# Down projection of 40 of 44 ffn tiles by one level of Strassen's algorithm, its products placed between units of gate and up

## The chip, the cores and the metric

The kernel runs on one core of a Trainium2 chip. The metric is the device time of one execution in microseconds; for the kernel before it is the median of three runs. A profile of one execution stands beside it. The engines are TensorE (PE, with its weight loads as PEld), VectorE (DVE), ScalarE (ACT), GpSimd (POOL) and SyncE (SP), which here only issues loads and stores.

## The reference

The kernel computes one encoder block on 512 tokens of width 2048 in float32: a norm, an input projection, two kinds of token mixing (Fourier and gated), an output projection, a second norm, a SwiGLU ffn of width 5632 and a last norm.

```python
h = rmsnorm(x, norm_mix); z = h @ w_in
y_f = fourier_mixer(z[..., :1024], w_fourier)
u, v = split(gelu(z[..., 1024:]))
y_g = spatial_gating_mixer(u, v, g_sgu, w_spatial, b_spatial)
x = x + concatenate([y_f, y_g], -1) @ w_out
h2 = rmsnorm(x, norm_ffn)
x = x + (silu(h2 @ w_gate) * (h2 @ w_up)) @ w_down
return rmsnorm(x, norm_final)
```

The change touches the last projection, `@ w_down`, and the order of the work around it.

## The kernel before

**Precision.** Every float32 product is carried by three passes of a shorter format. An operand is split into hi, a cast on ScalarE, and lo, the rest, a subtraction on VectorE (`split`, L169 to L171, and `weights`, L66 to L78). `mm3` (L80 to L84) issues hi times hi, one hi times lo, and lo times hi into the same bank; so its three lines carry nearly all matmuls in the profile.

**Weights.** All large weights come in units of 128x1024 (512 KB). `weights` loads a unit into a tile called raw, and splits it into hi and lo. Each of the three has three buffers, which all units share in turn.

**Stages ahead of the ffn.** The input projection (stages a, v and u), the mixing, and the output projection (stage o) run ahead of it. The residual x lies in eight slots of the pool `spool`, 24 slots of 4 KB a partition; `x2c(m, n)` is its block of token tile m (128 tokens, four of them) and column block n (512 columns, four of them). The normalized input of the ffn, transposed, is kept as 16 pairs h2hi and h2lo.

**The ffn.** Its width is 44 tiles of 128. `gate_up(f)` (L486) makes one tile of the activation, transposed: gate is 16 k tiles of 3 matmuls into one bank, two units of weights; then up in the same way. VectorE scales gate by `rg`, the reciprocal norm of each token, ScalarE takes the tanh, VectorE forms the product with it; up is scaled by `ru`, half of rg, and GpSimd multiplies both (L493 to L498). The tile is split into hi and lo (L500).

**Down.** Tiles are taken in groups of four (`GROUPS`, L35): for each of four column blocks two units of w_down are loaded, and for each of four token tiles `down` (L505) accumulates four tiles in one bank, 12 matmuls, which VectorE adds to x at L511. The groups are ten of four tiles and two of two. `gate_up` runs one tile ahead of the group's down. The last group's weights are split into slots of their own; its sixteen blocks are followed by the squares on ScalarE, the product with norm_final on GpSimd, the last norm and the stores (L536 to L554).

**What sets the order.** SP's queue is kept as the code writes it. On the other engines a planner puts the instructions in an order of its own, which keeps the dependencies; each engine then executes its queue in that order. A tile waits until a buffer of its pool is free. The banks of the accumulator are eight, all from one pool.

Of the kernel before, what the change touches and what calls it, by code (L numbers as in the profile page):

```python
# [16 lines left out]
P = 128  # L17
D = 2048  # model width
S = 512  # tokens
KT = D // P  # k tiles of the model width  # L20
NT = S // P  # token tiles
HEADS = 8  # fourier heads, and gmlp heads
GW = HEADS * P  # width of a head group
DFF = 5632
FT = DFF // P  # tiles of the ffn width
EPS = 1e-6
U = 1024  # columns of a unit of weights

# the tile of u behind which v is ready for the gate
# [3 lines left out]
# ffn tiles per accumulation of the down projection; the last group is small, so that  # L33
# little is left to do behind the last matmul
GROUPS = [4] * 10 + [2, 2]  # L35
# [3 lines left out]
def encoder_block(ctx, tc, a, out):  # L39
    """The block on one core.  # L40

    A float32 product is carried by float32r passes: an operand is hi + lo exactly, hi its
    leading 12 bits and lo the other 12, and hi*hi + hi*lo + lo*hi is accumulated in float32.
    """
# [3 lines left out]
    # loads and stores in the order written here  # L48
# [4 lines left out]
    spool = ctx.enter_context(tc.tile_pool(name="s", bufs=24))  # L53
# [12 lines left out]
    def weights(src, name, pieces=1):  # L66
        """A unit of weights, as hi and lo."""
# [12 lines left out]
    def mm3(ps, lhs, rhs, first, last):  # L80
        """ps += lhs.T @ rhs, both as (hi, lo)."""
        mm(ps, lhs[0], rhs[0], start=first, stop=False)  # L82
        mm(ps, lhs[0], rhs[1], start=False, stop=False)  # L83
        mm(ps, lhs[1], rhs[0], start=False, stop=last)  # L84

# [4 lines left out]
    # the tensor engine's clock rises with its use: keep it at work until the first operands are there  # L90
# [9 lines left out]
    def rsqrt(dst, ssq, scale, shape, name):  # L100
        """dst = 1 / sqrt(ssq * scale + eps), with a Newton step."""
# [39 lines left out]
    def by_token(pss, units, nk, lhs, name, per_k=None, then=()):  # L141
        """Four banks, one for each token tile: sum over k of lhs(k).T @ the unit's columns.
        then[kk] is other work, to be issued behind unit kk."""
# [15 lines left out]
    def by_feature(ps, units, nk, rhs, name):  # L159
        """One bank: the transpose of rhs times 128 columns of weights."""  # L160
# [12 lines left out]
    def pair(name, width=U):  # L173
        """hi and lo of `width` columns."""
        if width == U:
            return slot(name + "_hi", F32R), slot(name + "_lo", F32R)
        t = slot(name, F32R, (P, 2, S))
        return t[:, 0, :], t[:, 1, :]

# [4 lines left out]
    yf = []  # mixed features, transposed, as (hi, lo)  # L184
# [15 lines left out]
    def fourier_classes(av, n, scaled):  # L200
        """The sums over the four token tiles that a DFT of 512 as 4 x 128 needs."""
# [25 lines left out]
    def fourier_tokens(h):  # L227
        u, v, y0, y2 = (both(x, head_columns(h)) for x in cls[h // 4])
        # real and imaginary parts of the DFT over the tokens, [feature, frequency]:
        # re of 4m+1, re of 4m+2, re of 4m | im of 4m, im of 4m+2, im of 4m+1  # L230
# [10 lines left out]
    def fourier_features(h):  # L241
        # over the head's features, and its weights
# [7 lines left out]
        for sign, op in ((1, ALU.add), (-1, ALU.subtract)):  # L250
            # frequencies 4m+1 and their negatives
# [23 lines left out]
    def fourier_weights(n):  # L275
        """cos and sin of the head features' DFT, times the heads' weights."""
# [9 lines left out]
    def token_squares():  # L286
        """1 / rms by token, on the token's partition."""
# [5 lines left out]
    def token_squares_everywhere():  # L293
        """1 / rms by token, on every partition."""
# [18 lines left out]
    # hT is made as it is needed  # L313
# [21 lines left out]
    def gelu2(z, s, dst):  # L335
        """dst = 2 gelu(z), by tanh; s holds z squared."""
# [32 lines left out]
    # of v, where v2 = 2 v  # L369
# [10 lines left out]
    # v's place, once vn is there  # L380
# [85 lines left out]
    rg = const.tile([P, S], F32, name="rg")  # L466
    ru = const.tile([P, S], F32, name="ru")

    def ffn_scales():
        """1 / rms by token, on every partition."""  # L470
# [6 lines left out]
        nc.vector.tensor_scalar_mul(ru, rg, 0.5)  # L477

# [4 lines left out]
    fss = const.tile([P, NT, 4], F32, name="fss")  # L483
    act = [None] * FT

    def gate_up(f):  # L486
        pg, pu = bank(f"g{f}"), bank(f"up{f}")
        by_feature(pg, a["w_gate"][f], KT, lambda k: h2[k], f"g{f}")
        if f == 0:
            ffn_scales()  # L490
        t = slot(f"ft{f}", F32, (P, 2, S))
        z, s = t[:, 0, :], t[:, 1, :]
        nc.vector.tensor_mul(z, pg, rg)  # L493
        nc.scalar.activation(s, z, AF.Tanh, scale=0.5)
        nc.vector.scalar_tensor_tensor(z, s, 1.0, z, op0=ALU.add, op1=ALU.mult)
        by_feature(pu, a["w_up"][f], KT, lambda k: h2[k], f"up{f}")
        nc.vector.tensor_mul(s, pu, ru)
        nc.gpsimd.tensor_tensor(out=z, in0=z, in1=s, op=ALU.mult)  # L498
        act[f] = pair(f"act{f}", S)
        split(z, act[f])  # L500

    def down_units(f0, size, n):
        return [weights(a["w_down"][(f0 + 2 * j) // 2][n], f"d{f0}_{n}_{j}") for j in range(size // 2)]

# [124 lines left out]
```

## Time and profile before

| what | value |
| --- | --- |
| median of 3 runs | 1940.79 us (1940.61 to 1940.95) |
| span of the profiled execution, first to last instruction | 1938.5 us |
| mean granted TensorE clock | 0.997 |
| read from HBM, written | 191.98 MB, 4.19 MB |
| DMA, share of 16 engines | 30% |
| loads of w_down | 84 + 4 of 512 KB |

The device time of the profiled execution itself is not recorded, only its span; the median of the runs is 2.3 us above it. In the profile's groups each row has a line, an engine, an operation, its tiles, a shape and a count; then the busy time in us, the mean of one in ns, and how long the engine sat idle just ahead of them and what ended that. TensorE overlaps its matmuls: a single one is shown with 389 ns, while they start about every 0.227 us, so times on TensorE are taken from the starts. Tiles whose names differ only in a number are one row: d is down, g gate, up up, act the split activation.

### The profile page before, as it was taken

How to read it: one execution, taken by the hardware profiler on the slowest of the kernel's cores; microseconds unless marked ns; L12 is line 12 of the kernel's file. 1: busy time of each engine (PE TensorE's matmuls, PEld its weight loads, DVE VectorE, ACT ScalarE, POOL GpSimd, SP SyncE). 2: the span in 40 equal slices, each digit the busy share in tenths (PEclk: the TensorE clock that was granted, in tenths of full speed). 3: DMA queues.
4: the chain of work that ended last, by engine and by line, in shares of the span. 5: the costliest groups of instructions: out<-in, count | busy, mean ns of one | idle time of the engine just before them, and what ended most of it. 6: DMA issues, size and time to landing. Idle time of an engine off the chain costs nothing.

```text
span 1938.5 us, 20697 instructions
## 1 busy us (share of the span) xinstructions
PE 1919.9 (99%) x8610; PEld 1593.7 (82%) x8610; DVE 866.2 (45%) x1006; ACT 544.1 (28%) x684; POOL 124.2 (6%) x96
## 2 busy tenths in 40 slices
PE   9999999999999999999999999999999999999996
PEld 8888888888888888888888888888888888888885
DVE  7555663333434334343444343443433433434447
ACT  6345532223322221222212222222222122222224
POOL 5001110000000000000000000000000000000003
PEclk9999999999999999999999999999999999999998
DMA  6223224423222323323233223232232232332332
GB/s 240 95 70 108 90 74 141 142 87 119 88 98 87 109 98 98 98 91 104 89 98 98 98 87 109 87 109 98 92 100 95 94 98 98 98 98 87 106 104 94
DMA packets 55965, 197.51 MB, mean 102 GB/s; under 512 B 6592, under 2 KB 6720, under 8 KB 55872
## 3 DMA queue, kind: packets, MB, share of 16 engines
q1 hardware_dynamic: 55584, 195.15, 30.2%
q8 instruction: 67, 1.10, 0.2%
q0 software_dynamic: 288, 1.05, 0.2%
q14 instruction: 26, 0.21, 0.0%
HBM read 191.98 MB, written 4.19 MB: 101 GB/s over the span
## 4 chain that ended last, share of the span: by engine, by line
PE 97%; DVE 1%; ACT 1%; DMA 0%; issue 0%; POOL 0%; SPq 0%; ACTq 0%; DVEq 0%
PE up L83 8%; PE g L82 8%; PE g L83 8%; PE up L82 8%; PE g L84 8%; PE up L84 8%; PE d L84 8%; PE d L83 8%; PE d L82 8%; PE o L84 3%; PE o L83 3%; PE o L82 3%; PE a L82 2%; PE a L83 2%; PE a L84 2%; PE v L82 1%
## 5 line engine op out<-in xcount | busy, mean ns | idle before, releaser
L82 PE MATMUL up<-h2hi,hi_up 128*128 128x512 f32 x704 | 274.0, 389 | 0.0
L83 PE MATMUL up<-h2lo,hi_up 128*128 128x512 f32 x704 | 273.9, 389 | 0.0
L82 PE MATMUL g<-h2hi,hi_g 128*128 128x512 f32 x704 | 273.9, 389 | 0.0
L84 PE MATMUL g<-h2hi,lo_g 128*128 128x512 f32 x704 | 273.9, 389 | 0.0
L83 PE MATMUL g<-h2lo,hi_g 128*128 128x512 f32 x704 | 273.9, 389 | 0.0
L84 PE MATMUL up<-h2hi,lo_up 128*128 128x512 f32 x704 | 273.9, 389 | 0.0
L82 PE MATMUL d<-hi_d,act 128*128 128x512 f32 x672 | 261.4, 389 | 0.0
L83 PE MATMUL d<-lo_d,act 128*128 128x512 f32 x672 | 261.4, 389 | 0.0
L84 PE MATMUL d<-hi_d,act 128*128 128x512 f32 x672 | 261.4, 389 | 0.0
L511 DVE TENSOR_TENSOR x<-d,x 128x512 f32<-128x512 f32 x192 | 131.4, 687 | 160.4 <-PE d L84 159.4
L77 DVE TENSOR_TENSOR lo_up<-raw_up,hi_up 128x1024 fp32r<-128x1024 f32 x88 | 141.7, 1610 | 127.8 <-ACT hi_up L76 127.8
L76 ACT CAST hi_g<-raw_g 128x1024 fp32r<-128x1024 f32 x88 | 92.8, 1054 | 367.8 <-PE g L83 144.7
L76 ACT CAST hi_d<-raw_d 128x1024 fp32r<-128x1024 f32 x84 | 88.6, 1055 | 382.2 <-PE d L84 242.8
L77 DVE TENSOR_TENSOR lo_g<-raw_g,hi_g 128x1024 fp32r<-128x1024 f32 x88 | 107.7, 1224 | 150.7 <-ACT hi_g L76 150.6
L76 ACT CAST hi_up<-raw_up 128x1024 fp32r<-128x1024 f32 x88 | 92.8, 1054 | 272.2 <-PE up L83 140.4
L77 DVE TENSOR_TENSOR lo_d<-raw_d,hi_d 128x1024 fp32r<-128x1024 f32 x84 | 114.5, 1363 | 97.3 <-ACT hi_d L76 97.3
L84 PEld LDWEIGHTS g<-h2hi,lo_g 128*128 128x128 f32 x704 | 132.1, 188 | 27.5
L82 PEld LDWEIGHTS up<-h2hi,hi_up 128*128 128x128 f32 x704 | 132.1, 188 | 27.5
L82 PEld LDWEIGHTS g<-h2hi,hi_g 128*128 128x128 f32 x704 | 132.1, 188 | 27.4
L84 PEld LDWEIGHTS up<-h2hi,lo_up 128*128 128x128 f32 x704 | 132.1, 188 | 27.4
L83 PEld LDWEIGHTS g<-h2lo,hi_g 128*128 128x128 f32 x704 | 132.1, 188 | 27.4
L83 PEld LDWEIGHTS up<-h2lo,hi_up 128*128 128x128 f32 x704 | 132.1, 188 | 27.3
(229 smaller groups left out, 2511.6 us busy)
## 6 DMA issues: line engine op xcount, KB each, us to landing
raw_g<-in_w_gate SPq DMA_DIRECT2D x88, 512.0 KB, 3.3
raw_up<-in_w_up SPq DMA_DIRECT2D x88, 512.0 KB, 3.3
raw_d<-in_w_down SPq DMA_DIRECT2D x84, 512.0 KB, 3.3
raw_o<-in_w_out SPq DMA_DIRECT2D x32, 512.0 KB, 3.3
raw_v<-in_w_v SPq DMA_DIRECT2D x16, 512.0 KB, 3.3
raw_u<-in_w_u SPq DMA_DIRECT2D x16, 512.0 KB, 3.4
raw_a<-in_w_a SPq DMA_DIRECT2D x15, 512.0 KB, 3.5
x<-in_x SPq DMA_DIRECT2D x8, 512.0 KB, 8.0
```

Of the source, the lines that this page charges most:

```text
L76: nc.scalar.copy(hi[:, c], raw[:, c])
L77: nc.vector.tensor_sub(lo[:, c], raw[:, c], hi[:, c])
L82: mm(ps, lhs[0], rhs[0], start=first, stop=False)
L83: mm(ps, lhs[0], rhs[1], start=False, stop=False)
L84: mm(ps, lhs[1], rhs[0], start=False, stop=last)
L511: nc.vector.tensor_add(x2c(m, n), ps, x2c(m, n))
```

## The change

Of the 44 ffn tiles the first 40 are taken in ten groups of four, called quads. A quad's contribution to x is a product of a 512x512 matrix (tokens by ffn) and a 512x2048 matrix. For each half of the columns (np_, 1024 wide) both are cut into 2x2 blocks, of 256 tokens by 256 ffn and of 256 ffn by 512 columns, and the 2x2 block product is formed by seven block products in place of eight (Winograd's form of Strassen's algorithm). `quad_down` yields after each product. Ahead of it VectorE forms sums of the left blocks (tile x) and, in place, of the weight blocks (r); both operands are split into hi and lo. Product 2 accumulates into product 1's banks and product 3 into product 5's. A value of products 1 and 2 goes to one output block, of 5 to another, and so on; what several output blocks share (products 1 and 6) is summed over all quads in `usum`, and `fold` adds it to or subtracts it from three of the four output blocks once, after the last quad.

`gate_up` becomes a generator that yields after each of its four units of weights. While the units of a quad run, one product of the quad before is run after each unit but the first; so the 14 products (two halves of seven) stand between 16 units of gate and up.

The activation is no longer split by tile; it stays float32 in two slots a quad. `rg` takes the place of the earlier `rstdB`, and the factor 0.5 of `ru` goes into the instruction that reads up. w_down of a quad is loaded into slots of `spool` (`down_loads`) rather than into raw. The pool has 25 slots. norm_final is loaded after the last quad. The last four tiles keep the plain form, as two groups of two.

```diff
-GROUPS = [4] * 10 + [2, 2]
+H = S // 2
+QUADS = 10
...
-    spool = ctx.enter_context(tc.tile_pool(name="s", bufs=24))
+    spool = ctx.enter_context(tc.tile_pool(name="s", bufs=25))
...
-    rg = const.tile([P, S], F32, name="rg")
-    ru = const.tile([P, S], F32, name="ru")
+    rg = rstdB
     def ffn_scales():
...
         nc.vector.tensor_copy(rg, ps)
-        nc.vector.tensor_scalar_mul(ru, rg, 0.5)
+    fss = const.tile([P, NT, 4], F32, name="fss")
+    act = [None] * FT
+    def gate_up(f, z):
+        pg, pu = bank(f"g{f}"), bank(f"up{f}")
+        s = small.tile([P, S], F32, tag="act", bufs=1, name=f"s{f}")
+        per = U // P
+        for ps, w, name in ((pg, a["w_gate"], "g"), (pu, a["w_up"], "up")):
+            for kk in range(KT // per):
+                hi, lo = weights(w[f][kk], f"{name}{f}_{kk}")
+                for j in range(per):
+                    k = kk * per + j
+                    c = slice(j * P, (j + 1) * P)
+                    mm3(ps, (hi[:, c], lo[:, c]), h2[k], k == 0, k == KT - 1)
+                if kk == 0:
+                    yield
+            if name == "g":
+                if f == 0:
+                    ffn_scales()
+                nc.vector.tensor_mul(z, pg, rg)
+                nc.scalar.activation(s, z, AF.Tanh, scale=0.5)
+                nc.vector.scalar_tensor_tensor(z, s, 1.0, z, op0=ALU.add, op1=ALU.mult)
+            else:
+                nc.vector.scalar_tensor_tensor(s, pu, 0.5, rg, op0=ALU.mult, op1=ALU.mult)
+                nc.gpsimd.tensor_tensor(out=z, in0=z, in1=s, op=ALU.mult)
+            yield
+    ORDER = (1, 2, 5, 6, 3, 7, 4)
+    usum = [slot(f"u{np_}", F32, (P, 2, S)) for np_ in range(2)]
+    for np_ in range(2):
+        nc.gpsimd.memset(usum[np_], 0.0)
+    def out_block(k, t, np_):
+        return x2c(2 * (k // 10 - 1) + t, 2 * np_ + k % 10 - 1)
+    def down_loads(q, np_):
+        r = {}
+        for k in (11, 21, 12, 22):
+            r[k] = slot(f"w{k}_{q}_{np_}")
+            nc.sync.dma_start(r[k], a["w_down"][2 * q + k // 10 - 1][2 * np_ + k % 10 - 1])
+            yield r
+    def quad_down(q, np_, A, loads):
+        A11, A21 = A[0][:, :, :H], A[0][:, :, H:]
+        A12, A22 = A[1][:, :, :H], A[1][:, :, H:]
+        x = None
+        ps = {}
+        r = {}
+        for i in ORDER:
+            name = f"{q}_{np_}_{i}"
+            if i == 5:
+                x = slot(f"x{q}_{np_}", F32, (P, 2, H))
+                nc.vector.tensor_sub(x, A21, A22)
+            elif i == 6:
+                nc.vector.tensor_sub(x, x, A11)
+            elif i == 3:
+                nc.vector.tensor_add(x, x, A12)
+            elif i == 7:
+                nc.vector.tensor_sub(x, A11, A21)
+            X = slot(f"X{name}", F32R, (P, 2, 2, H))
+            split({1: A11, 2: A12, 4: A22}.get(i, x), (X[:, 0], X[:, 1]))
+            if i in (1, 2, 5, 6):
+                r = next(loads)
+            if i == 5:
+                nc.vector.tensor_add(r[11], r[11], r[12])
+            elif i == 6:
+                nc.vector.tensor_add(r[11], r[11], r[22])
+            elif i == 7:
+                nc.vector.tensor_add(r[12], r[12], r[22])
+            elif i == 4:
+                nc.vector.tensor_add(r[11], r[11], r[21])
+            raw = r[{1: 11, 2: 21, 5: 11, 6: 11, 3: 22, 7: 12, 4: 11}[i]]
+            hi = wpool.tile([P, U], F32R, tag="hi", name=f"hi_d{name}")
+            lo = wpool.tile([P, U], F32R, tag="lo", name=f"lo_d{name}")
+            split(raw, (hi, lo))
+            more = {2: 1, 3: 5}.get(i)
+            ps[i] = ps[more] if more else [bank(f"d{name}_{t}") for t in range(2)]
+            for j in range(2):
+                c = slice(j * S, (j + 1) * S)
+                for t in range(2):
+                    l = slice(t * P, (t + 1) * P)
+                    w = (hi[:, c], lo[:, c])
+                    p = ps[i][t]
+                    mm(p, X[:, 0, j, l], w[0], start=j == 0 and not more, stop=False, skip_group_check=True)
+                    mm(p, X[:, 0, j, l], w[1], start=False, stop=False, skip_group_check=True)
+                    mm(p, X[:, 1, j, l], w[0], start=False, stop=j == 1, skip_group_check=True)
+            for t in range(2):
+                if i in (1, 6):
+                    d = usum[np_][:, t, :]
+                else:
+                    d = out_block({2: 11, 5: 22, 3: 12, 7: 21, 4: 21}[i], t, np_)
+                nc.vector.tensor_add(d, ps[i][t], d)
+                if i == 7:
+                    d = out_block(22, t, np_)
+                    nc.vector.tensor_sub(d, d, ps[i][t])
+            yield
+    def fold():
+        for np_ in range(2):
+            for t in range(2):
+                for k in (12, 21, 22):
+                    d = out_block(k, t, np_)
+                    nc.vector.tensor_tensor(d, d, usum[np_][:, t, :], op=ALU.add if k == 21 else ALU.subtract)
+    def downs(q, A):
+        for np_ in range(2):
+            yield from quad_down(q, np_, A, down_loads(q, np_))
+    def run(work):
+        next(work, None)
+    def chain(works):
+        for w in works:
+            yield from w
+    pending = iter(())
+    for q in range(FT // 4):
+        A = [slot(f"act{q}_{i}", F32, (P, 2, S)) for i in range(2)]
+        for i, _ in enumerate(chain(gate_up(4 * q + f, A[f // 2][:, f % 2, :]) for f in range(4))):
+            if i > 0:
+                run(pending)
+        pending = downs(q, A)
+        if q == QUADS:
+            fold()
+            rest = A
     gB = [slot(f"gB{i}") for i in range(2)]
     for i in range(2):
         nc.sync.dma_start(gB[i], a["norm_final"][:, i * U : (i + 1) * U].partition_broadcast(P))
-    fss = const.tile([P, NT, 4], F32, name="fss")
-    act = [None] * FT
-    def gate_up(f):
-        pg, pu = bank(f"g{f}"), bank(f"up{f}")
-        by_feature(pg, a["w_gate"][f], KT, lambda k: h2[k], f"g{f}")
-        if f == 0:
-            ffn_scales()
-        t = slot(f"ft{f}", F32, (P, 2, S))
-        z, s = t[:, 0, :], t[:, 1, :]
-        nc.vector.tensor_mul(z, pg, rg)
-        nc.scalar.activation(s, z, AF.Tanh, scale=0.5)
-        nc.vector.scalar_tensor_tensor(z, s, 1.0, z, op0=ALU.add, op1=ALU.mult)
-        by_feature(pu, a["w_up"][f], KT, lambda k: h2[k], f"up{f}")
-        nc.vector.tensor_mul(s, pu, ru)
-        nc.gpsimd.tensor_tensor(out=z, in0=z, in1=s, op=ALU.mult)
-        act[f] = pair(f"act{f}", S)
-        split(z, act[f])
-    def down_units(f0, size, n):
-        return [weights(a["w_down"][(f0 + 2 * j) // 2][n], f"d{f0}_{n}_{j}") for j in range(size // 2)]
-    def down(f0, size, m, n, units, ps):
-        for j in range(size):
-            hi, lo = units[j // 2]
-            c = slice((j % 2) * S, (j % 2 + 1) * S)
-            t = slice(m * P, (m + 1) * P)
-            mm3(ps, both(act[f0 + j], t), (hi[:, c], lo[:, c]), j == 0, j == size - 1)
-        nc.vector.tensor_add(x2c(m, n), ps, x2c(m, n))
-    done = 0
-    f0 = 0
-    for i, size in enumerate(GROUPS[:-1]):
-        # a tile ahead, so that the last one's activation is not waited for
-        ahead = f0 + size + 1 if i + 2 < len(GROUPS) else FT
-        while done < ahead:
-            gate_up(done)
-            done += 1
-        for n in range(4):
-            units = down_units(f0, size, n)
-            for m in range(NT):
-                down(f0, size, m, n, units, bank(f"d{f0}_{m}_{n}"))
-        f0 += size
-    size = GROUPS[-1]
+    last = []
+    for i in range(2):
+        for f in range(2):
+            p = pair(f"al{i}_{f}", S)
+            split(rest[i][:, f, :], p)
+            last.append(p)
     fr = const.tile([P, NT], F32, name="fr")
     fs = const.tile([P, NT], F32, name="fs")
+    def down(fs_, m, n, units):
+        ps = bank(f"l{fs_[0]}_{m}_{n}")
+        t = slice(m * P, (m + 1) * P)
+        for j, f in enumerate(fs_):
+            mm3(ps, both(last[f], t), both(units[n], slice(j * S, (j + 1) * S)), j == 0, j == len(fs_) - 1)
+        nc.vector.tensor_add(x2c(m, n), ps, x2c(m, n))
+    for n in range(4):
+        units = {n: weights(a["w_down"][FT // 2 - 2][n], f"dk{n}")}
+        for m in range(NT):
+            down((0, 1), m, n, units)
     units = []
     for n in range(4):
         raw = wpool.tile([P, U], F32, tag="raw", name=f"raw_l{n}")
-        nc.sync.dma_start(raw, a["w_down"][f0 // 2][n])
+        nc.sync.dma_start(raw, a["w_down"][FT // 2 - 1][n])
         p = pair(f"dl{n}")
         split(raw, p)
-        units.append([p])
+        units.append(p)
     for m in range(NT):
         o = [slot(f"o{m}_{i}") for i in range(2)]
         oc = [o[n // 2][:, (n % 2) * S : (n % 2 + 1) * S] for n in range(4)]
         for n in range(4):
-            down(f0, size, m, n, units[n], bank(f"d{f0}_{m}_{n}"))
+            down((2, 3), m, n, units)
             squares(m, n, fss[:, m, n : n + 1])
-            last = m == NT - 1 and n == 3
-            (nc.vector if last else nc.gpsimd).tensor_tensor(
+            final = m == NT - 1 and n == 3
+            (nc.vector if final else nc.gpsimd).tensor_tensor(
                 out=oc[n], in0=x2c(m, n), in1=gB[n // 2][:, (n % 2) * S : (n % 2 + 1) * S], op=ALU.mult
             )
```

## The prediction

> **What bounds the kernel now.** I read the page first: the busy shares, the line of the granted clock, and the chain that ended last.
>
> ```profile
> span 1938.5 us, 20697 instructions
> PE 1919.9 (99%) x8610; PEld 1593.7 (82%) x8610; DVE 866.2 (45%) x1006; ACT 544.1 (28%) x684; POOL 124.2 (6%) x96
> PEclk9999999999999999999999999999999999999998
> PE 97%; DVE 1%; ACT 1%; DMA 0%; issue 0%; POOL 0%; SPq 0%; ACTq 0%; DVEq 0%
> ```
>
> TensorE carries 97% of the chain at the full clock. A modelled busy time can hide gaps, so I checked what TensorE waits for (the view of waits, TensorE alone) and its rate (the timeline, from the first matmul of one gate tile to the first of its up tile, 48 matmuls later).
>
> ```profile
> PE u L84 <- DVE lo_u L77: 1.2, 1, 1.2
> PE warm L93 <- DVE eps L96: 1.1, 1, 1.1
> PE a L82 <- ACT hhi L131: 0.7, 1, 0.7
> ...
> 1030.53 0.39 PE L82 MATMUL g<-h2hi,hi_g 128*128 128x512 f32 x1
> 1041.41 0.39 PE L82 MATMUL up<-h2hi,hi_up 128*128 128x512 f32 x1
> ```
>
> All its recorded waits are 3.0 us, none in the ffn. 48 matmuls start in 10.88 us: 0.2267 us each. The ffn is therefore paid by the count of matmuls, and every other engine is free as long as it is in time. How near they are to being late is in a table of stretches: microseconds, then the busy time of PE (count), PEld, DVE, ACT, POOL, then clock and DMA.
>
> ```profile
> 846.50:977.00 130.50, 130.50 (x577) 108.09 (x576) 54.15 (x56) 29.86 (x33) 5.16 (x4) 1.00 0.30 97
> 10.00:40.00 30.00, 30.00 (x133) 24.82 (x132) 30.00 (x20) 22.16 (x34) 23.34 (x14) 1.00 0.74 272
> 250.00:260.00 10.00, 10.00 (x46) 8.26 (x45) 8.69 (x11) 4.09 (x7) 2.58 (x2) 1.00 0.01 2
> 1880.00:1890.00 10.00, 10.00 (x46) 8.28 (x45) 9.39 (x12) 4.87 (x6) 1.30 (x1) 1.00 0.36 120
> ```
>
> The first row is one turn of four ffn tiles: 16 units of gate and up and 8 of down, 24 matmuls each, 576 in all. VectorE is busy in 41% of it. The others show TensorE at the same rate (133 in 30 us is 0.2256 each) while VectorE is busy for 100%, 87% and 94% of the stretch.
>
> **What goes from TensorE.** These groups are down's work; L83 and L84 have the same counts.
>
> ```profile
> L82 PE MATMUL d<-hi_d,act 128*128 128x512 f32 x672 | 261.4, 389 | 0.0
> L82 PE MATMUL d<-dl_hi,act 128*128 128x512 f32 x32 | 12.4, 389 | 0.0
> L511 DVE TENSOR_TENSOR x<-d,x 128x512 f32<-128x512 f32 x192 | 131.4, 687 | 160.4 <-PE d L84 159.4
> L77 DVE TENSOR_TENSOR lo_d<-raw_d,hi_d 128x1024 fp32r<-128x1024 f32 x84 | 114.5, 1363 | 97.3 <-ACT hi_d L76 97.3
> L77 DVE TENSOR_TENSOR lo_g<-raw_g,hi_g 128x1024 fp32r<-128x1024 f32 x88 | 107.7, 1224 | 150.7 <-ACT hi_g L76 150.6
> L171 DVE TENSOR_TENSOR act<-ft,act 128x512 fp32r<-128x512 f32 x44 | 29.8, 678 | 0.0
> L76 ACT CAST hi_d<-raw_d 128x1024 fp32r<-128x1024 f32 x84 | 88.6, 1055 | 382.2 <-PE d L84 242.8
> L170 ACT CAST act<-ft 128x512 fp32r<-128x512 f32 x44 | 27.4, 623 | 55.0 <-POOL ft L498 55.0
> ```
>
> Down is 3 x 704 = 2112 matmuls. In a turn the 192 become 2 column halves x 7 products x 12 (two k tiles, two token tiles, three passes) = 168. The last four ffn tiles keep theirs. Ten turns save 240 matmuls of the same shape: 240 x 0.2267 = **54.4 us**. I take the whole of it, because nothing else is on the chain there. A new turn is then 16 x 5.44 + 14 x 2.72 = 125.1 us.
>
> **What VectorE and ScalarE get, per turn.** Splits of weights rise from 8 to 14: 6 x 1.224 = 7.3 us (the plain length, from lo_g). Splits of the left operand go from 4 to 14 of 128x512: 10 x 0.678 = 6.8. The 8 sums of left blocks read two SBUF operands like that split: 8 x 0.68 = 5.4. The 8 sums of weight blocks have lo_g's shape: 9.8. Evacuations rise from 16 to 32 (two for each product, four for the seventh's): 16 x 0.687 = 11.0. Together 40.3 us on top of 54.15: VectorE stands at 94.5 of 125.1 us, **76%**. ScalarE gets 6 x 1.055 + 10 x 0.623 = 12.6 us on 29.86, 34%. Neither is a bound by its sum. No row has a block read as two runs of 256: between the row's 0.678 and twice it, 0 to 9.5 us more a turn; I take 0, since the element count is the row's. The product with 0.5 and rg in one instruction replaces the one with ru at the same shape; I cost it at nothing, and 0.1 us either way would be hidden. A split that meets POOL's product takes longer:
>
> ```profile
> 1052.49 0.69 DVE L497 TENSOR_TENSOR ft<-up,ru 128x512 f32<-128x512 f32 x1 [3.31 <-PE up L84]
> 1053.39 2.30 DVE L77 TENSOR_TENSOR lo_up<-raw_up,hi_up 128x1024 fp32r<-128x1024 f32 x1 [0.21 <-ACT hi_up L76]
> ...
> 1053.33 1.29 POOL L498 TENSOR_TENSOR ft<-ft 128x512 f32<-128x512 f32 x1 [63.99 <-DVE ft L497]
> ```
>
> 2.30 against 1.22 is 1.08 us, four times a turn; this stays and is in the 54.15. The two memsets on POOL come before the ffn's first product and are hidden by a whole turn of gate and up; bounded by 0 and two rows of POOL at 1.29 us, they are 0 here.
>
> **The new waits.** hi and lo have three buffers each, now used in the order unit, product, unit. A buffer that comes free lets ScalarE and VectorE begin the operand that TensorE wants 5.44 + 2.72 = 8.16 us later. The chain to fill it is cast 1.05 + split 1.22, and at worst a pair of evacuations (1.38) and a sum of weights (1.22) stand ahead: 4.9 us. The seventh product has two evacuations more: 6.3 us. Both are under 8.16. Product 2 adds to product 1's banks and product 3 to product 5's, so TensorE must wait until the earlier value is read; queued behind that matmul is all of TensorE, but at least one unit (5.44 us) lies between and the reading takes 1.38. An evacuation in VectorE's queue waits for TensorE to end a product, and the splits behind it wait too. How such orders come out is in the timeline of VectorE.
>
> ```profile
> 1006.25 0.69 DVE L511 TENSOR_TENSOR x<-d,x 128x512 f32<-128x512 f32 x1 [2.03 <-PE d L84]
> 1008.70 1.22 DVE L77 TENSOR_TENSOR lo_d<-raw_d,hi_d 128x1024 fp32r<-128x1024 f32 x1 [1.76 <-ACT hi_d L76]
> 1009.84 0.68 DVE L511 TENSOR_TENSOR x<-d,x 128x512 f32<-128x512 f32 x1
> 1010.44 1.22 DVE L77 TENSOR_TENSOR lo_d<-raw_d,hi_d 128x1024 fp32r<-128x1024 f32 x1
> ```
>
> The code writes all four evacuations of a column block ahead of the next block's splits; here the next split runs ahead of the last two evacuations. So the order on the engine follows readiness, not the text, and I expect evacuations not to hold up splits that are ready. I take 0 for stalls inside the turns. From the other side, one of the recorded 1.2 us waits at each of 140 products would be 168 us, and from 54.4 / 140 = 0.39 us a product nothing is left of the gain.
>
> SP's queue keeps the written order: the same 88 loads of down, but 80 go to slots of the common pool, between the loads of gate and up. A load without a free slot would hold the next gate load behind it. Of 25 slots 8 are x, 2 the common sums, 2 to 4 activations, 4 the weight blocks, 1 the running sum: 6 to 8 are left for split operands and the next blocks, and a split operand is needed two deep. The waits of before bear on how far SP runs ahead:
>
> ```profile
> SPq L73 <- DVE lo_d L77: 450.7, 81, 8.7
> ...
> ACT dl_hi L170 <- DMA raw_l<-in_w_down: 5.5, 3, 2.9
> raw_d<-in_w_down SPq DMA_DIRECT2D x84, 512.0 KB, 3.3
> ```
>
> The loads wait for buffers, and hardly anything waits for a load. I take 0; at the other end 3.3 us of landing at each of the 20 halves is 66 us.
>
> **The end.** The fold adds 12 x 0.69 = 8.3 us to VectorE around the last unit, where it was busy for 9.39 of 10 us; most of it can run before, as the sums of the first half are final a half turn earlier. The last 32 evacuations follow, and their stretch is set by VectorE:
>
> ```profile
> 1901.00:1912.00 11.00, 11.00 (x50) 9.13 (x49) 6.38 (x12) 6.12 (x15) 8.36 (x7) 1.00 0.01 1
> 1912.00:1925.00 13.00, 10.85 (x48) 8.63 (x46) 12.22 (x26) 8.11 (x22) 8.42 (x7) 1.00 0.47 162
> ```
>
> Between, 4.6 us are free. The fold costs 0 to 8.3 us; I take 2. The load of norm_final goes to the end, behind the last gate and up loads, and its reader comes some 20 us later; 0.
>
> **Sum.** 1938.5 - 54.4 + 2 = 1886.1 us of span. The median of the runs, 1940.79, is 2.3 above the span, and that stays: **1888.5 us**.
>
> **Rivals.** *Heavy steps stall.* The seventh product has 2.75 us of evacuations, and the step's work is 7.8 us (a unit's split, four evacuations, two splits, two sums) plus up to 1.8 behind an up product (0.69 for its reading, 1.08 beside POOL), against 8.16. If its two extra evacuations (1.38 us) reach TensorE at each of 20 halves, 28 us come back: 1916. For it: 76% leaves little in such a step. Against it: VectorE at 100% over 30 us without one lost matmul.
>
> *Slower: VectorE's order.* If a product's evacuations stand ahead of the next unit's split in VectorE's queue, that split starts only after TensorE ends the product: 1.38 + 1.22 = 2.6 us, less two matmuls that need no lo (0.45), so 2.15 us at each of 140 products, 301 us, about 2190; it decides from 0.39 us a product. For it: the evacuations double and every one waits for TensorE. Against it: the order in the timeline above. The Trainium skill (TensorE: Matmul & The Clock Gate, section "Architectural detail") says that VectorE's queue is strictly first in, first out, so nothing passes a waiting evacuation; the idle 2.03 us ahead of one at 1006.25 agrees. The same page, section "HAM oscillation", says that gaps over some 3.4 us bring the halved clock; no gap of 2.15 us would, and here only the stretch after the last matmul shows a lower clock.
>
> *Nothing gained.* The matmuls do go, by the count; but stalls near 0.39 us a product would leave 1937 to 1945.
>
> **Chances.** Forecast 0.72, heavy steps 0.14, slower 0.11, nothing 0.03. A difference of 0.2% (3.9 us) is about what these runs can tell. Faster 0.86, same 0.03, slower 0.11. The forecast's own ends are 1886 (a fold that is hidden) and 1897 (8.3 us for it and a few waits); the range reaches over the heavy steps, 1884 to 1918, and leaves out the slower case and the one without gain.
>
> **What would show it.** TensorE's count falls by 240 and its share stays at 99%; a turn takes 125 us with VectorE near 95 us busy; the waits of TensorE stay at a few us. A wait of TensorE on lo or on X with a count near 140 would prove the slower rival, one near 20 the heavy steps; waits of ScalarE on loads of w_down would speak for the slots. It would also be wrong if VectorE's new instructions were well over their neighbours' rows.

## The result, and the profile after

The changed kernel takes **2016.49 us** (median of 4 runs, 2015.28 to 2017.54); the kernel before, run beside it, takes 1940.7 us. The ratio is **1.0392, interval 1.0377 to 1.0406**: 3.9% slower, where 1888.5 us was forecast. The profiled execution spans 2014.5 us at a mean granted clock of 0.972 (before: 1938.5 us at 0.997). Two experiments below turn the same change into a gain of 2.8%, so the result is 130 us of loss laid over a gain that is there.

The page of the kernel after:

```profile
span 2014.5 us, 20956 instructions
PE 1917.3 (95%) x8370; PEld 1573.0 (78%) x8370; DVE 1220.0 (61%) x1497; ACT 658.7 (33%) x844; POOL 130.2 (6%) x98
...
PE 92%; DVE 5%; ACT 1%; issue 1%; DMA 0%; SPq 0%; POOL 0%; ACTq 0%; DVEq 0%
...
w<-in_w_down SPq DMA_DIRECT2D x80, 512.0 KB, 4.5
```

The count of matmuls fell from 8610 to 8370, the 240 that were forecast. But their busy time fell by only 2.6 us, and the share of the span went from 99% to 95%: TensorE now idles, and some of its matmuls take longer than before. The chain now has 5% on VectorE, against 1% before. The waits of TensorE (engine and line, what ended the wait, us in total, times, longest) say where:

```profile
PE d L577 <- ACT hi_d L170: 59.6, 20, 3.6
PE d L578 <- DVE lo_d L171: 18.2, 20, 1.2
PE u L84 <- DVE lo_u L77: 1.2, 1, 1.2
```

Two new rows of 20 each, 77.8 us. L577 is the first pass of a block product, which wants the cast weights hi_d; L578 is the second, which wants lo_d. Of 140 products 20 wait, so two in each turn of 14: one in each half of the columns. The timeline of all engines around such a wait (start, duration, engine, line, operation, operands; in brackets the idle time before it and what ended that) shows what ScalarE was doing:

```profile
988.54 0.39 PE L82 MATMUL g<-h2hi,hi_g 128*128 128x512 f32 x1
...
990.90 0.62 ACT L170 CAST X<-act 128x512 fp32r<-128x512 f32 x1 [6.03 <-POOL act L503]
...
999.20 0.39 PE L84 MATMUL g<-h2hi,lo_g 128*128 128x512 f32 x1
999.62 0.69 DVE L498 TENSOR_TENSOR act<-g,rstdB 128x512 f32<-128x512 f32 x1 [10.12 <-PE g L84]
1000.23 1.28 DVE L171 TENSOR_TENSOR X<-act,X 128x512 fp32r<-128x512 f32 x2
1000.35 0.63 ACT L499 ACTIVATE s<-act 128x512 f32<-128x512 f32 x1 [8.82 <-DVE act L498]
1000.88 1.03 ACT L170 CAST hi_d<-w 128x1024 fp32r<-128x1024 f32 x1
...
1001.97 0.73 PE L577 MATMUL d<-hi_d,X 128*128 128x512 f32 x2 [2.38 <-ACT hi_d L170]
...
1002.64 1.22 DVE L171 TENSOR_TENSOR lo_d<-w,hi_d 128x1024 fp32r<-128x1024 f32 x1
...
1003.91 0.80 PE L578 MATMUL d<-lo_d,X 128*128 128x512 f32 x1 [1.21 <-DVE lo_d L171]
```

At 999.20 the last matmul of a gate tile starts. VectorE, idle for 10.12 us until then, scales the tile (L498); ScalarE, idle for 8.82 us, takes its tanh (L499), and only then casts the weights of the next product, which TensorE is already waiting for. The cast needs nothing of the gate. Of the three buffers of hi two hold the gate's own units, and the one that it fills was last read by the unit ahead of this gate, which ended when the gate began, at 988.54. Its weights were there long before, as the timeline of SP's queue shows:

```profile
969.70 0.42 SPq L529 DMA_DIRECT2D w<-in_w_down  x1
```

The load was issued 31 us ahead of the cast and such loads land after 4.5 us. So the cast was ready for some 12 us, ScalarE was idle, and the cast still came after the tanh: it stands behind it in ScalarE's queue. The waits of ScalarE say that this is the rule for such a tanh, and that loads of w_down are not what it waits for (of w_down's loads only three of the last group are in this view):

```profile
ACT s L499 <- DVE act L498: 217.7, 21, 12.8
...
ACT dl_hi L170 <- DMA raw_l<-in_w_down: 5.5, 3, 2.9
```

ScalarE stands for 217.7 us ahead of 21 tanhs. The order of the queue around the same place of an earlier turn, the tanh of tile 12, as the two programs have it (the position in the program's own list for ScalarE; the second column is that of the experiment e1_touch, below). Both traces have ScalarE's instructions in this order, with this tanh at 861.21 us and 836.51 us:

```text
after                               e1_touch
                                    368  X2_0_1   (left operand, product 1)
...
380  hi_g12_0                       381  hi_g12_0
381  hi_g12_1                       382  hi_g12_1
382  X2_0_1                         383  hi_d2_0_1
383  X2_0_2                         384  X2_0_2
384  tanh s12  (waits for the gate) 385  X2_0_5
385  hi_d2_0_1 (weights, product 1) 386  hi_up12_0
386  X2_0_5                         ...
387  hi_up12_0                      390  tanh s12
```

The Trainium skill (TensorE: Matmul & The Clock Gate, section "Architectural detail") calls ScalarE's queue strictly first in, first out; the 8.82 us of idle time with a ready cast behind the tanh agree.

Not all that the next product needs is held back: in the first column the cast of its left operand (X2_0_1) stands ahead of the tanh, and so does that for the product after it (X2_0_2; its counterpart in the timeline is at 990.90). Of what the product's first pass reads, only the cast of the weights stands behind.

The idle time is not the whole loss. This is TensorE's timeline at the first of the 20 stalls (589.48 is the wait for lo_d):

```profile
584.76 0.39 PE L84 MATMUL g<-h2hi,lo_g 128*128 128x512 f32 x1
587.53 1.22 PE L577 MATMUL d<-hi_d,X 128*128 128x512 f32 x2 [2.38 <-ACT hi_d L170]
589.48 0.80 PE L578 MATMUL d<-lo_d,X 128*128 128x512 f32 x1 [0.72 <-DVE lo_d L171]
590.07 0.63 PE L579 MATMUL d<-hi_d,X 128*128 128x512 f32 x1
590.50 0.63 PE L578 MATMUL d<-lo_d,X 128*128 128x512 f32 x1
...
593.48 0.63 PE L579 MATMUL d<-hi_d,X 128*128 128x512 f32 x1
593.91 0.48 PE L82 MATMUL up<-h2hi,hi_up 128*128 128x512 f32 x1
594.23 0.40 PE L83 MATMUL up<-h2lo,hi_up 128*128 128x512 f32 x1
594.46 0.40 PE L84 MATMUL up<-h2hi,lo_up 128*128 128x512 f32 x1
```

From 590.07 to 593.91 nine matmuls start 0.427 us apart, against 0.227 elsewhere; the granted clock is 0.50 there (a table behind the last experiment shows it). From 584.76 to 593.91 it does the work of 13 spacings, 2.95 us, in 9.15 us. This one stall costs 6.2 us: 3.1 of recorded waits and 3.1 of half clock and start-up. A table of stretches (length; busy time and count of PE, PEld, DVE, ACT, POOL; clock; DMA share; GB/s) gives one whole turn:

```profile
1004.20:1141.50 137.30, 129.22 (x553) 105.47 (x553) 89.11 (x105) 41.41 (x50) 5.48 (x4) 0.97 0.26 92
```

137.3 us where 125.1 was forecast: 12.2 us for two stalls, 6.1 each. VectorE is busy for 65% of it, so this is not an engine with too much work.

### The profile page after: what moved, and what is told of

The parts are those of the page before. It is cut to its first block, busy times and chain, and to the rows that moved or that the text cites. A ratio compares the mean times of both kernels' runs of the same rounds, so it can differ in the third digit from the quotient of the medians.

```text
span 2014.5 us, 20956 instructions
## 1 busy us (share of the span) xinstructions
PE 1917.3 (95%) x8370; PEld 1573.0 (78%) x8370; DVE 1220.0 (61%) x1497; ACT 658.7 (33%) x844; POOL 130.2 (6%) x98
## 4 chain that ended last, share of the span: by engine, by line
PE 92%; DVE 5%; ACT 1%; issue 1%; DMA 0%; SPq 0%; POOL 0%; ACTq 0%; DVEq 0%
PE up L82 8%; PE up L84 8%; PE up L83 8%; PE g L84 8%; PE g L82 8%; PE g L83 8%; PE d L578 7%; PE d L579 7%; PE d L577 6%; PE o L84 3%; PE o L82 3%; PE o L83 3%; PE v L82 1%; PE v L84 1%; PE v L83 1%; PE a L84 1%
## 5 line engine op out<-in xcount | busy, mean ns | idle before, releaser
L577 PE MATMUL d<-hi_d,X 128*128 128x512 f32 x560 | 227.2, 412 | 59.6 <-ACT hi_d L170 59.6
L170 ACT CAST hi_d<-w 128x1024 fp32r<-128x1024 f32 x140 | 146.9, 1049 | 383.3 <-PE g L83 165.6
L171 DVE TENSOR_TENSOR lo_d<-w,hi_d 128x1024 fp32r<-128x1024 f32 x140 | 203.5, 1454 | 106.6 <-ACT hi_d L170 104.0
L578 PE MATMUL d<-lo_d,X 128*128 128x512 f32 x560 | 237.8, 425 | 18.2 <-DVE lo_d L171 18.2
L579 PE MATMUL d<-hi_d,X 128*128 128x512 f32 x560 | 233.6, 417 | 0.0
L577 PEld LDWEIGHTS d<-hi_d,X 128*128 128x128 f32 x560 | 110.3, 200 | 90.6 <-ACT hi_d L170 68.1
L498 DVE TENSOR_TENSOR act<-g,rstdB 128x512 f32<-128x512 f32 x44 | 30.4, 692 | 220.6 <-PE g L84 220.5
L578 PEld LDWEIGHTS d<-lo_d,X 128*128 128x128 f32 x560 | 114.3, 204 | 52.8 <-DVE lo_d L171 28.7
L503 POOL TENSOR_TENSOR act<-act,s 128x512 f32<-128x512 f32 x44 | 61.2, 1390 | 1451.9 <-DVE s L502 776.1
```

The source lines that it names most:

```text
L170: nc.scalar.copy(dst[0], src)
L171: nc.vector.tensor_sub(dst[1], src, dst[0])
L577: mm(p, X[:, 0, j, l], w[0], start=j == 0 and not more, stop=False, skip_group_check=True)
L578: mm(p, X[:, 0, j, l], w[1], start=False, stop=False, skip_group_check=True)
L579: mm(p, X[:, 1, j, l], w[0], start=False, stop=j == 1, skip_group_check=True)
```

## The experiments

**The theories.** *A, the order of handing out.* The planner gives out the slots of the common pool in the order in which the code writes them. A quad's activation tile takes its slot at its first write, which is the scaling of a whole gate (L498). The slots that the next product needs (its left operand X, its weights) are written behind that, so they are planned behind it, and in the end so is the cast. *B, load.* VectorE and ScalarE have too much to do near these products; the prediction's heavy steps, in another place. *C, the clock.* A part of the loss is TensorE's halved clock, not the waits themselves. The planner's reason stands in no trace; only the order that it made does, and that order shows the weight cast behind the tanh, not the operand's. So A is tested by changing what it would act on.

| run | what it is | median us | ratio to before (interval) | span | clock |
| --- | --- | --- | --- | --- | --- |
| after | the change | 2016.49 | 1.0392 (1.0377 to 1.0406) | 2014.5 | 0.972 |
| e1_touch | both activation tiles written early | 1886.30 | 0.9720 (0.9704 to 0.9736) | 1884.6 | 0.997 |
| e2_touch_first | only the first of them | 1961.93 | 1.0111 (1.0091 to 1.0131) | 1960.4 | 0.980 |
| e3_no_weight_sums | after, without the weight sums | 2017.79 | 1.0399 (1.0378 to 1.0420) | 2016.1 | 0.972 |
| e4_filler | after, 16 idle matmuls in each gap | 1978.52 | 1.0197 (1.0176 to 1.0217) | 1976.3 | 0.997 |
| e5_gate_late | product written ahead of the scaling | 1885.61 | 0.9719 (0.9691 to 0.9748) | 1882.9 | 0.997 |
| e6_touch_24 | e1_touch with 24 slots | 1885.58 | 0.9719 (0.9691 to 0.9748) | 1883.9 | 0.997 |
| e7_touch_more_vector | e1_touch, more work on VectorE | 1889.35 | 0.9739 (0.9710 to 0.9767) | 1887.9 | 0.997 |
| e8_filler_4 | after, 4 idle matmuls in each gap | 2015.77, one run | | 2014.0 | 0.973 |
| e9_filler_9 | after, 9 idle matmuls in each gap | 1989.75, one run | | 1988.0 | 0.991 |

**e1_touch** writes one column of each activation tile as soon as it is declared. Nothing reads these zeros; only the place of the tile's first write changes.

```diff
         A = [slot(f"act{q}_{i}", F32, (P, 2, S)) for i in range(2)]
+        for i in range(2):
+            nc.gpsimd.memset(A[i][:, 0, :1], 0.0)
```

> Both activation tiles of a quad get a small write at the quad's top, so that their slots are handed out before the gate is done. Theory A (slots of the common pool are handed out in the written order, and the activation tile, first written behind the gate, holds back the product's operand, so that ScalarE's queue has the weight cast behind the gate's tanh): TensorE's waits in the ffn fall from 78 us to under 8, the mean granted clock returns to 0.997, and the time is 1885 to 1897 us. Theory B (VectorE has too much to do in the turns): the tiny writes change nothing, 2005 to 2020 us.

Measured: 1886.30 us, 130 us below the change and 2.8% below the kernel before. It beats both kernels. The waits of TensorE that are left:

```profile
PE u L84 <- DVE lo_u L77: 1.2, 1, 1.2
PE warm L93 <- DVE eps L96: 1.1, 1, 1.1
PE a L84 <- DVE hlo L132: 0.9, 1, 0.9
PE a L82 <- ACT hhi L131: 0.8, 2, 0.5
```

None is in the ffn. The table of stretches, one turn:

```profile
845.00:970.10 125.10, 125.10 (x554) 103.58 (x553) 90.22 (x105) 41.93 (x48) 5.36 (x6) 1.00 0.29 101
```

TensorE is busy throughout at the full clock. The timeline of ScalarE at the second half's start, where after the change TensorE would wait for the second product, shows the casts ahead of the tanh here too:

```profile
1017.82 1.05 ACT L170 CAST hi_d<-w 128x1024 fp32r<-128x1024 f32 x1
...
1025.61 1.05 ACT L170 CAST hi_d<-w 128x1024 fp32r<-128x1024 f32 x1 [3.65 <-PE g L83]
1026.56 0.63 ACT L499 ACTIVATE s<-act 128x512 f32<-128x512 f32 x1
```

TensorE begins the second product at 1025.58. Its cast (1017.82) and that for the third (1025.61, when TensorE ends a unit and a buffer of hi comes free) both run ahead of the tanh at 1026.56. The wait of ScalarE ahead of the tanhs has shrunk from 217.7 us:

```profile
ACT s L499 <- DVE act L498: 3.9, 11, 1.4
```

Two column writes a quad move no work off any engine (VectorE has 1497 instructions in both kernels). So B, with too much work as its cause, falls.

**e2_touch_first** writes only the first tile, `A[0]`, early.

```diff
+        nc.gpsimd.memset(A[0][:, 0, :1], 0.0)
```

> Only the first of a quad's two activation tiles is written early. Theory A: the ten stalls at the first product of the first half go, the ten at the second product of the second half stay (about 4.2 us of wait each) with their share of the half clock: 1945 to 1965 us. Theory B: 2005 to 2020 us.

Measured: 1961.93 us. The waits of TensorE:

```profile
PE d L577 <- ACT hi_d L170: 35.8, 10, 3.6
PE d L578 <- DVE lo_d L171: 7.9, 10, 0.9
```

Ten of the twenty stalls are gone, those of the first half; the ten of the second, whose activation tile is still first written late, stay with their 3.6 us. Each of the two tiles thus has its own stall. The ten that stay cost 1960.4 - 1884.6 = 75.8 us, 7.6 each, more than the 6.5 on average after the change (129.9 us over 20). Of that the waits are 4.4, against 3.9; for the rest see the clock behind the last experiment.

**e3_no_weight_sums** leaves out the eight sums of weight blocks a quad (L556 to L563), so that the products are of the plain blocks, to take 9.8 us of every turn from VectorE.

```diff
-            if i == 5:
-                nc.vector.tensor_add(r[11], r[11], r[12])
-            elif i == 6:
-                nc.vector.tensor_add(r[11], r[11], r[22])
-            elif i == 7:
-                nc.vector.tensor_add(r[12], r[12], r[22])
-            elif i == 4:
-                nc.vector.tensor_add(r[11], r[11], r[21])
```

> The sums of weight blocks are left out (8 a quad, 98 us of VectorE in all), so that the products are of the plain blocks. Theory A: the stalls are in ScalarE's order and stay; 2008 to 2018 us. Theory B: with 8% of VectorE's work in a turn gone the stalls shrink; below 1975 us.

Measured: 2017.79 us, no different from the change, with the same waits (these lines lie eight higher in this kernel):

```profile
PE d L569 <- ACT hi_d L170: 59.6, 20, 3.6
PE d L570 <- DVE lo_d L171: 18.7, 20, 1.2
```

With 9.8 us less of VectorE's work in every turn the stalls stay as they were, so its load is not what makes them.

**e4_filler** leaves the order as it is, and fills each of the 20 gaps with 16 matmuls of the stalled size; they write the bank of the next up tile (`pus[f]`), which that tile's first matmul overwrites. The first quad has no product beside it and gets none. They lie in the gap, where TensorE has nothing to do, and keep it running.

```diff
+FILL = 16
...
+    def filler(f):
+        for _ in range(FILL if f >= 4 else 0):
+            mm(pus[f], h2[0][0][:, :P], h2[0][0], start=True, stop=True, skip_group_check=True)
...
+            if i == 1 or i == 9:
+                filler(4 * q + i // 4)
             if i > 0:
                 run(pending)
```

> Sixteen more matmuls of 512 columns, whose result is overwritten, stand in TensorE's queue in each of the 20 gaps (320 in all, 3.6 us a gap). Theory A with the clock: the gap is set by the gate's end, tanh and cast and doesn't get longer, the clock stays at 1.00 through the ffn, and the some 51 us of half clock come back: 1960 to 1972 us. If the half clock costs nothing: 2012 to 2020. If the gap is work that TensorE could have had: 2080 to 2090.

Measured: 1978.52 us, 38 us less than the change although 320 matmuls are added, and the clock is back at 0.997. The waits of TensorE (L580 and L581 of the three kernels with filler are L577 and L578 of the change):

```profile
PE d L581 <- DVE lo_d L172: 11.5, 20, 0.9
```

Only waits of 0.6 us on average are left, and no matmul starts 0.43 us apart any more. So C holds: 38 us of the loss were the clock. The size was missed, since 1960 to 1972 us were expected: at half clock for 51 us in excess (101 us of it, from the mean clock: (0.997 - 0.972) x 2014.5 / 0.5) not all is loss, because a part of the half-clock time lies in the gap itself, where nothing runs. The rest of this kernel against e1_touch is 1976.3 - 1884.6 = 91.7 us: 320 x 0.2267 = 72.5 for the added matmuls, 11.5 for the waits, and 7.7 us that I can't attribute.

**e5_gate_late** makes no early write, but moves the place where the code writes the scaling and the tanh: `gate_up` yields after the gate's second unit, so the product between is written ahead of the scaling.

```diff
-                if kk == 0:
+                if kk == 0 or name == "g":
                     yield
...
                 nc.gpsimd.tensor_tensor(out=z, in0=z, in1=s, op=ALU.mult)
-            yield
+                yield
```

> No early write; instead the gate's scaling and tanh are written behind the product that follows the gate, so that this product's slots are handed out ahead of the activation tile's. Theory A: the casts stand ahead of the tanh in ScalarE's queue, the 20 stalls go, 1885 to 1900 us. If the early write of E1 helped for another reason than the order (something on GpSimd, a shift in time): 2000 to 2020 us.

Measured: 1885.61 us, the same as e1_touch. In ScalarE's queue the cast of product 1 now stands three places ahead of that tanh (383 and 386). TensorE has no wait left in the ffn, although ScalarE still stands idle ahead of the tanhs:

```profile
ACT s L499 <- DVE act L498: 101.2, 21, 5.2
```

So it is not the tanh's wait that costs, but what stands behind it. This edit by itself does not tell A from a simpler reason, since it writes the cast itself ahead of the tanh; e1_touch leaves both where they are written and moves only the first write of the tile.

**e6_touch_24** is e1_touch with one slot less, the number before the change.

```diff
-    spool = ctx.enter_context(tc.tile_pool(name="s", bufs=25))
+    spool = ctx.enter_context(tc.tile_pool(name="s", bufs=24))
```

> As E1, with 24 slots in the common pool in place of 25. Theory A (the order of handing out, not the number): within 3 us of E1, 1884 to 1890 us. Theory C (the pool is short of slots, and the early write only shifted the shortage): a slot less brings stalls back, over 1900 us.

(The theory C of this expectation is a shortage of slots, not the clock.) Measured: 1885.58 us. With the early write a slot less costs nothing, so the early write did not just move a shortage. The change itself with more slots was not run.

**e7_touch_more_vector** gives VectorE two products more of 128x512 with every block product, to find how much cover is left.

```diff
+            for n in range(2):
+                j = small.tile([P, S], BF16, tag="sq", bufs=1, name=f"idle{name}_{n}")
+                nc.vector.tensor_mul(j, rg, rg)
```

> As E1, with two more products of 128x512 on VectorE behind each block product, whose results nobody reads: 28 x 0.69 = 19 us a turn, so that VectorE is busy for some 92% of it. If what the prediction said holds (VectorE's work is hidden while it is in time): 1886 to 1896 us. Theory B in its weak form (VectorE is near its limit): stalls at the heavy products, over 1910 us.

Measured: 1889.35 us. The table of stretches, two turns one behind the other:

```profile
845.00:970.10 125.10, 124.99 (x552) 103.23 (x551) 124.03 (x166) 40.70 (x49) 8.40 (x6) 1.00 0.29 101
970.10:1095.20 125.10, 125.01 (x552) 103.22 (x551) 100.22 (x125) 42.00 (x49) 7.74 (x6) 1.00 0.29 101
```

In the first VectorE is busy for 99% of the turn, in the second for 80%, and both take 125.1 us: added work is put off, not waited for. In the ffn TensorE waits for VectorE twice, 2.3 us in all, both times for the reading of an accumulator (L585). So VectorE at 99% of a turn costs next to nothing where the queues are in a good order; the change lost 130 us with VectorE at 65%.

**e8_filler_4 and e9_filler_9** repeat e4_filler with 4 and 9 matmuls, one run each, to see how short a pause still halves the clock.

```diff
-FILL = 16
+FILL = 4
```

> Four filler matmuls a gap in place of sixteen, so TensorE idles 0.9 us less in each: some 3.4 us in the first half's gap and 4.2 in the second's, each still broken by one or two matmuls. If the half clock needs a quiet time of about the gap's whole length, some of the 20 clock drops go and others stay: the time lies between 1978 and 2016 us, with the number of drops between. If any wait of 2 us drops the clock, all 20 stay and the time is 2010 to 2018.

> Nine filler matmuls a gap: 2.0 us less idle, 2.2 and 3.1 us left. If quiet time of some 3.4 us is needed, no drop is left and the time is as with sixteen, 1974 to 1982 us. If a wait of 2 us is enough, drops stay in most gaps and the time is above 1990.

Measured: 2015.77 us with 4. The waits of TensorE there:

```profile
PE d L580 <- ACT hi_d L171: 41.5, 20, 2.7
PE d L581 <- DVE lo_d L172: 19.2, 20, 1.2
```

And 1989.75 us with 9:

```profile
PE d L581 <- DVE lo_d L172: 21.1, 20, 1.2
PE d L580 <- ACT hi_d L171: 18.9, 20, 1.5
```

With 4 the recorded waits are 60.7 us, 3.0 a stall in two parts, and the clock falls at 19 of the 20 stalls; the time lies where "any wait of 2 us" put it. With 9 they are 40.0 us, and it falls at 7 of the 20: at seven of the ten of the second half (1.5 and 0.9 us of wait) and at none of the first (0.3 and 1.2). That time lies between the two that were expected.

The traces say more than a length of pause. A table of stretches around the first and the third stall of the change (the last three numbers are the granted clock, the DMA share and GB/s):

```profile
583.85:587.26 3.41, 1.30 (x6) 0.75 (x4) 2.07 (x4) 1.34 (x2) 0.00 (x0) 1.00 0.00 0
587.26:594.09 6.83, 5.83 (x13) 4.15 (x14) 6.30 (x8) 3.35 (x5) 0.00 (x0) 0.50 0.23 78
594.09:597.50 3.41, 3.41 (x17) 2.79 (x16) 2.92 (x3) 1.05 (x1) 0.00 (x0) 1.00 0.01 2
723.80:727.21 3.41, 0.73 (x2) 0.30 (x2) 3.41 (x6) 2.19 (x4) 0.00 (x0) 1.00 0.00 0
727.21:730.62 3.41, 2.88 (x7) 2.30 (x8) 3.41 (x5) 2.45 (x3) 0.00 (x0) 0.50 0.05 11
730.62:734.04 3.42, 3.42 (x17) 2.79 (x16) 2.98 (x5) 1.10 (x2) 0.00 (x0) 1.00 0.39 146
```

In the first stall the clock falls at 587.26, 2.11 us into the first wait (585.15 to 587.53), before any second wait. Within each of the traces with stalls all its changes in the ffn lie whole steps of 3.41 us apart, and half clock lasts one step or two. After the change ten of the 20 half-clock stretches last 3.41 us and ten 6.83; in e2_touch_first nine of ten last 6.83. That is 1.4 us more at half clock for each stall, which fits the 0.6 us by which its stalls are dearer beyond their waits. I added up TensorE's recorded waits in each step of these traces (after, e2, e4, e8, e9): in the 56 steps at whose end the clock fell they came to 1.6 to 3.3 us, in those after which it stayed full to 1.55 or less, with one exception of 1.94. By this it is the idle time within a step that counts, wherever the step happens to begin. At the one stall of e8 that kept the clock, the two waits of 1.48 and 1.21 us fell into two steps.

## Why the prediction was wrong

**What held.** The sum itself was right, and e1_touch shows it with the stalls gone: 1884.6 us of span against 1886.1.
- The 240 matmuls of 0.2267 us went, 54.4 us. A turn without stalls takes the forecast 125.1 us. (The terms add up to 1888.4 us, where 1888.5 was written.)
- VectorE was put at 94.5 us a turn and has 90.2; ScalarE at 42.5 and has 41.9. The sum adds whole durations, which overlap where instructions stand close behind one another: L498 above starts at 999.62, lasts 0.69, and the next starts 0.61 later. A left block read as two runs of 256, costed at nothing, costs next to nothing: the splits of X and the sums take 0.68 to 0.69 us each in e1_touch.
- Waits for an accumulator's earlier value don't appear among the waits of TensorE after the change or in e1_touch, nor late loads of the quads' w_down among those of ScalarE.
- The fold, taken as 2 us, and all else that was taken as nothing come to 0.5 us together (1884.6 less 1938.5 - 54.4).

**What failed: the step on the new waits.** It had two parts that were both taken as 0. The first said that "the order on the engine follows readiness, not the text", from a timeline in which a split passed evacuations (of its column block only one, at 1009.84, not two: by the starts on TensorE the block ends at 1008.77); so a cast would start when its buffer came free, 8.16 us ahead of its use. This held for 120 of 140 products. In the other 20 the planned order put a cast behind a tanh that waits for TensorE's own next result, and an engine that executes its queue in order could not mend it: the cast of the example ran at 1000.88, 12.3 us after its buffer came free and 1.3 us after TensorE had gone idle. Where the sum had 0 us, these stalls cost 129.9. The second part counted how many slots the pool has. e1_touch and e2_touch_first show that it matters when a tile of the pool is first written, and the prediction never asked for that; that the planner goes from there to the cast by the order of handing out slots is argued and not shown. The code had what the question needs: of the three kinds of tiles that newly share the pool, one is first written at the end of a gate, and the two others are wanted right after it.

**The second miss: the clock.** It was dismissed, with the price of a stall taken as the wait alone. 20 waits of 3.9 us would have been 77.8 us; measured are 2014.5 - 1884.6 = 129.9. Of the 52 us on top, e4_filler gives back 38 by holding the clock, and the other 14, 0.7 a stall, were not taken apart. I set the rule of the Trainium skill (TensorE: Matmul & The Clock Gate, section "HAM oscillation"), gaps over some 3.4 us, against gaps of 2.15 us and concluded that they are safe. Here the clock fell 2.11 us into an unbroken wait of 2.38 us (the first stall), at 19 of 20 stalls with 3.0 us of wait and at 7 of 20 with 2.0. The rule's length is too long for this kernel, and the measurement decides.

**The rivals.** *Heavy steps stall* is not it, though it would have named the right count: the prediction said that a count near 20 would prove it. The 20 stalls are at the first product of one half and the second of the other, not at the seventh, taking work from VectorE (e3_no_weight_sums) leaves them as they are, and adding work without them (e7_touch_more_vector) costs 3 us. *Slower: VectorE's order* had the sign and the kind of cause, an instruction that waits for TensorE ahead of one that TensorE needs; but the waiting one was ScalarE's tanh, not VectorE's evacuations, and the evacuations cost next to nothing (0.5 us for everything but the stalls). *Nothing gained* was not it either: the 54 us are gained and 130 are lost over them.

## What to carry to other kernels

When tiles of several kinds share one pool, find for each when it is first written. Here the one that is first written behind a late result went with a cast behind that result in ScalarE's queue, and a write of one column at an early place removed the loss. Counting an engine's load says nothing of this; look for an instruction that waits for the bound engine's next result, and ask what that engine wants from the queue behind it. Price a stall of TensorE above its wait: 3.9 us of wait cost 6.5 us here, because matmuls at half clock follow.

## What was not expected of the hardware

- The clock halved at stalls with 3.9 us of recorded waits 20 times in 20, with 3.0 us 19 times, with 2.0 us 7 times, with 0.6 us never. In these traces it changed only at steps of 3.41 us and fell after steps with 1.6 us or more of idle TensorE; half clock then lasted 3.41 or 6.83 us.
- The same kind of stall can differ in price by where it falls in these steps: the ten of e2_touch_first cost 7.6 us each, the twenty of the change 6.5 on average. TensorE was at half clock for some 6.5 us for each of the ten and 5.1 for each of the twenty.
- Adding 320 matmuls made a kernel 38 us faster (e4_filler against the change).
